# Attention products of 256 columns: from whole fp32 operands to two parts each and three single-pass matmuls

## The chip, the cores and the metric

One core of a Trainium2 chip runs the whole program. The metric is the device time of one execution in microseconds (us), as the median of several runs; one further execution is taken by the hardware profiler, and all rows below come from that one.

## The reference, cut to what matters

A decoder trunk of two layers over 256 tokens with a model width of 2048 and 16 heads of 128. Layer 0 has 8 stick-breaking heads and 8 dilated-window heads, layer 1 has 16 forgetting heads. All arrays are float32.

```python
def forgetting_attention(q, k, v, log_f):          # layer 1, all 16 heads
    s = einsum('bqhd,bkhd->bhqk', qblk, k) * scale
    s = s + cq[..., None] - c[:, :, None, :]
    s = where(kpos[None, :] <= qpos[:, None], s, -inf)
    return einsum('bhqk,bkhd->bqhd', softmax(s), v)

def stick_breaking_attention(q, k, v):             # layer 0, heads 0 to 7
    z = einsum('bqhd,bkhd->bhqk', qblk, k) * scale
    w = exp(log_sigmoid(z) + suffix)               # strictly causal
    return einsum('bhqk,bkhd->bqhd', w, v)
# layer 0, heads 8 to 15: a softmax over a mixture of dilated windows

for i in range(DEPTH):
    a = rmsnorm(h, attn_norm[i])
    h = h + mixer(a)                               # w_in, attention, w_out
    h = h + conv_ffn(rmsnorm(h, ffn_norm[i]), ...) # w_up, conv, w_down
    gate = sigmoid(rmsnorm(h, ple_norm[i]) @ w_ple_gate[i])
    h = h + gate * (p[i] @ w_ple[i])
return rmsnorm(h, final_norm)
```

## The kernel before

All activations lie in SBUF with features on the partitions and the 256 tokens as columns. The weights (453 MB) are streamed from HBM once. They are cut into 882 units, mostly of 4 blocks of 128x256 numbers. For each unit ScalarE rounds the raw weights to the single-pass type float32r (the high part, L176) and VectorE subtracts that from the raw weights (the low part, L177). The activations have two such parts as well. A product is then three single-pass matmuls of 256 columns (high by high, high by low, low by high; `PARTS`, L206 and L215), so a unit of four blocks is 24 matmuls. Units are split three ahead of their use (`LOOK`), into four buffers. In the value projection (`gemm_v`, L249) the roles are swapped: the activations are the stationary operand and the weights stream.

The heads are taken in pairs, eight pairs in each layer. `head_pair` emits four units each for q, k and v. Each unit ends in `tick()`, and small pieces of work are put between units by `defer(n, fn)`, which runs `fn` n units later. For each pair three such pieces run, while the next pair's projections stream:

- `first`: the scores. Of each head the causal blocks are one product of 128 columns (L435 in `sb_first`, L480 in `sm_first`) and one of 256 columns (L438, L482). They take q and k whole, as float32. In layer 1 a bias product of 384 columns in float32r comes before them (L478).
- `second`, four or five units later: `sb_second` (suffix sums by L456 to L464, single-pass, then Exp on ScalarE at L467) or `sm_second` (six transposes of 128 columns by TensorE at L517, then one copy to SBUF by ScalarE at L519).
- `attend`, two units later: the products of weights and values, again one of 128 columns (L526) and one of 256 (L529) for each of the two heads, all whole.

The values are copied out of PSUM by ScalarE with the row norm as a factor (L618, L585), the scores' q and k by VectorE (L590, L593). `t2_tile` gives one of six buffers of 128x512 floats. The engines' queues are in order: TensorE runs the scores exactly between the units where `defer` put them, and ScalarE and VectorE run the attention's steps between the splits of weights.

A float32 matmul is recorded as two instructions, each of which is a weight load (PEld) and a matmul (PE); a float32r matmul is recorded as one of each.

Of the kernel before, what the change touches and what calls it, by code (L numbers as in the profile page):

```python
# [17 lines left out]
P = 128  # L18
D = 2048
S = 256  # L20
# [84 lines left out]
def trunk(ctx: ExitStack, tc: tile.TileContext, xT, pT, pos, gains, conv, bf, cst, wst, out):  # L105
# [17 lines left out]
    acc = cpool.tile([P, 2, S], F32, name="acc")  # L123
    rb = cpool.tile([P, S], F32, name="rb")
    rq = cpool.tile([P, S], F32, name="rq")
    rT = cpool.tile([P, 2], F32, name="rT")

    root = cpool.tile([P, 2], F32, name="root")
    nc.gpsimd.memset(root, -0.5)

    ident = ct[:, C_ID:C_ID + 128]
# [62 lines left out]
    def defer(n, fn):  # L194
        later.append((at["tick"] + n, fn))
# [233 lines left out]
        nc.vector.tensor_add(out=x[:32], in0=x[:32], in1=sw)  # L429


    def sb_first(q, k):
        sc = at_tile("scs")
        for j in range(2):
            nc.tensor.matmul(sc[:, 1, j * P:(j + 1) * P], lhsT=k[:, j, 128:256], rhs=q[:, j, 128:256],  # L435
                             start=j == 0, stop=True, skip_group_check=True)
        for j in range(2):
            nc.tensor.matmul(sc[:, 0, j * S:(j + 1) * S], lhsT=k[:, j, 0:128], rhs=q[:, j, :],  # L438
                             start=j == 0, stop=True, skip_group_check=True)
        z, e = t3_tile("z"), t3_tile("e")  # L440
        for i, (a, b) in enumerate(((0, 256), (256, 384))):
            msk = ct[:, C_MSB + a:C_MSB + b].unsqueeze(1).to_broadcast([P, 2, b - a])
            nc.vector.tensor_add(out=z[:, 2 * a:2 * b].rearrange("p (j c) -> p j c", j=2),
                                 in0=sc[:, i, 0:2 * (b - a)].rearrange("p (j c) -> p j c", j=2), in1=msk)
        nc.vector.scalar_tensor_tensor(out=e, in0=z, scalar=-1.0, in1=z, op0=ALU.mult, op1=ALU.min)
        nc.scalar.activation(out=e, in_=e, func=AF.Exp)
        nc.scalar.activation(out=e, in_=e, func=AF.Ln, bias=1.0)
        nc.vector.scalar_tensor_tensor(out=e, in0=z, scalar=0.0, in1=e, op0=ALU.max, op1=ALU.add)
        eh, el = t3_tile("eh", (P, 768), F32R), t3_tile("el", (P, 768), F32R)
        nc.scalar.copy(out=eh, in_=e)  # L450
        nc.vector.tensor_sub(out=el, in0=e, in1=eh.bitcast(F32))
        return z, e, eh, el

    def sb_second(z, e, eh, el):
        sp = at_tile("sps")
        nc.tensor.matmul(sp[:, 0, :], lhsT=trir[:, 1, :], rhs=eh[:, 0:512],  # L456
                         start=True, stop=False, skip_group_check=True)
        for i, x in enumerate((eh, el)):
            nc.tensor.matmul(sp[:, 1, 0:256], lhsT=trir[:, 1, :], rhs=x[:, 512:768],
                             start=i == 0, stop=i == 1, skip_group_check=True)  # L460
            nc.tensor.matmul(sp[:, 0, :].rearrange("p (j c) -> p j c", j=2)[:, :, 128:256],
                             lhsT=trir[:, 0, :], rhs=x[:, 512:768].rearrange("p (j c) -> p j c", j=2),
                             start=False, stop=False, skip_group_check=True)
        nc.tensor.matmul(sp[:, 0, :], lhsT=trir[:, 1, :], rhs=el[:, 0:512],  # L464
                         start=False, stop=True, skip_group_check=True)
        nc.vector.tensor_sub(out=z, in0=z, in1=sp.rearrange("p a b -> p (a b)")[:, :768])
        nc.scalar.activation(out=e, in_=z, func=AF.Exp)  # L467
        return e

    SEG = ((0, 128), (128, 384))  # L470

    def sm_first(q, k, fox):
        sc = at_tile("scs")
        for j in range(2):
            if fox is not None:
                c2, sel, cq, h0 = fox
                lh = sel[:, h0 + j:h0 + j + 1].to_broadcast([P, P])
                nc.tensor.matmul(sc[:, j, 0:384], lhsT=lh, rhs=c2, start=True, stop=False,  # L478
                                 skip_group_check=True)
            nc.tensor.matmul(sc[:, j, 0:128], lhsT=q[:, j, 0:128], rhs=k[:, j, 0:128],  # L480
                             start=fox is None, stop=True, skip_group_check=True)
            nc.tensor.matmul(sc[:, j, 128:384], lhsT=q[:, j, 128:256], rhs=k[:, j, :],  # L482
                             start=False, stop=True, skip_group_check=True)
        s, pe = t3_tile("s", (P, 2, 384)), t3_tile("pe", (P, 2, 384))
        if fox is None:
            msk = ct[:, C_MDL:C_MDL + 384].unsqueeze(1).to_broadcast([P, 2, 384])
            nc.vector.tensor_add(out=s, in0=sc[:, :, :384], in1=msk)
        else:
            for j in range(2):
                for t, (a, b) in enumerate(SEG):  # L490
                    nc.vector.scalar_tensor_tensor(
                        out=s[:, j, a:b], in0=sc[:, j, a:b], scalar=cq[:, t, h0 + j:h0 + j + 1],
                        in1=ct[:, C_MFX + a:C_MFX + b], op0=ALU.add, op1=ALU.add)
        mx = work.tile([P, 2, 2], F32, name="mx", tag="mx", bufs=2)
        sm = work.tile([P, 2, 2], F32, name="sm", tag="sm", bufs=2)
        rsm = work.tile([P, 2, 2], F32, name="rsm", tag="rsm", bufs=2)
        for t, (a, b) in enumerate(SEG):
            nc.vector.tensor_reduce(out=mx[:, t, :], in_=s[:, :, a:b], axis=AX.X, op=ALU.max,
                                    negate=True)
        for j in range(2):  # L500
            for t, (a, b) in enumerate(SEG):
                nc.scalar.activation(out=pe[:, j, a:b], in_=s[:, j, a:b], func=AF.Exp,
                                     bias=mx[:, t, j:j + 1], accum_out=sm[:, t, j:j + 1])
        nc.vector.reciprocal(out=rsm, in_=sm)
        for t, (a, b) in enumerate(SEG):
            for j in range(2):
                nc.vector.tensor_scalar_mul(out=pe[:, j, a:b], in0=pe[:, j, a:b],
                                            scalar1=rsm[:, t, j:j + 1])
        return pe, s

    def sm_second(pe, s):

        sp = at_tile("sps")
        for j in range(2):
            for i in range(3):
                o = sp[:, 0, j * S + i * P:j * S + (i + 1) * P] if i < 2 else sp[:, 1, j * P:(j + 1) * P]
                nc.tensor.transpose(out=o, in_=pe[:, j, i * P:(i + 1) * P], identity=ident)  # L517
        w = s.rearrange("p a b -> p (a b)")
        nc.scalar.copy(out=w, in_=sp.rearrange("p a b -> p (a b)")[:, :768])  # L519
        return w  # L520

    def attend(hp, w, v, dst):
        av = at_tile("avp")
        for j in range(2):
            js = slice(j * P, (j + 1) * P)
            nc.tensor.matmul(av[:, 0, j * S + 128:(j + 1) * S], lhsT=v[:, 1, js],  # L526
                             rhs=w[:, 512 + j * P:512 + (j + 1) * P], start=j == 0, stop=False,
                             skip_group_check=True)
            nc.tensor.matmul(av[:, 0, j * S:(j + 1) * S], lhsT=v[:, 0, js], rhs=w[:, j * S:(j + 1) * S],  # L529
                             start=False, stop=True, skip_group_check=True)  # L530
        parts(dst[:, 2 * hp:2 * hp + 2], av[:, 0, :].rearrange("p (j s) -> p j s", j=2))


# [42 lines left out]
    def head_pair(l, hp, act, dst, st):  # L576
        q = work.tile([P, 2, S], F32, name="q", tag="qkv", bufs=2)
        k = work.tile([P, 2, S], F32, name="k", tag="qkv", bufs=2)
        v = work.tile([P, 2, S], F32, name="v", tag="v", bufs=1)
        full = _cuts(KT)  # L580
        if l % 2 == 1 and hp == 0:
            ps = at_tile("psv")
            gemm_vf(ps, act, l)
            for t in range(2):
                nc.scalar.activation(out=v[:, t, :], in_=ps[:, t, 0:S], func=AF.Copy,  # L585
                                     scale=rT[:, t:t + 1])
            st["fox"] = forget_gates(l, ps)
        ps = mm_tile("psq")
        gemm(ps, act, "w_in", l, hp * 256, full)
# [5 lines left out]

        def first():
            if l % 2 == 0 and hp < 4:
                a = sb_first(q, k)
                defer(5, lambda: second(lambda: sb_second(*a)))
            else:  # L600
                a = sm_first(q, k, st["fox"] + (2 * hp,) if l % 2 == 1 else None)
                defer(4, lambda: second(lambda: sm_second(*a)))

        def second(fn):
# [3 lines left out]
        if l % 2 == 0 and hp >= 4:  # L608
            rope(q)
            rope(k)  # L610

        defer(late + (2 + (l % 2 == 0 and hp >= 4) if hp == 7 or (l % 2 == 1 and hp == 0) else 4), first)
        if l % 2 == 1 and hp == 0:
            return
        ps = mm_tile("psv")
        gemm_v(ps, act, l, 2 * D + hp * 256)
        for i in range(2):
            nc.scalar.activation(out=v[:, i, :], in_=ps[:, i, :], func=AF.Copy, scale=rT[:, i:i + 1])  # L618

    def ffn_group(l, g, g0, act, hid):  # L620
        c = [t2_tile("yg"), t2_tile("yv")]
# [206 lines left out]
```

## Time and profile before

| | us |
|---|---|
| median of three runs | 2422.91 (2422.68 to 2423.42) |
| the profiled execution's own time | 2423.48 |
| its span, first to last instruction | 2421.7 |
| TensorE matmuls busy | 2407.1 (99%) |
| VectorE busy | 1581.5 (65%) |
| ScalarE busy | 1227.9 (51%) |
| granted TensorE clock, share of 2.4 GHz | 0.998 |

A matmul's recorded duration is a latency: the next one starts long before it ends. What a matmul costs the stream is the spacing of the ends, and the chain of waits gives that: each of its pieces is a stretch of one kind of work with a count, and the length over the count is the spacing.

### The profile page before, as it was taken

The numbers are of one execution on the slowest core, as the hardware profiler recorded it, in microseconds if no ns is written. First come the engines' busy times: TensorE is split into PE (matmuls) and PEld (weight loads), VectorE is DVE, ScalarE is ACT, GpSimd is POOL, SyncE is SP. The second block draws the span as 40 slices with busy tenths as digits, with TensorE's granted clock in tenths as the row PEclk, the third lists the DMA queues.
The fourth block names the chain that finished last, engine by engine and source line by source line (L and its number), as shares of the span: only waits on it lengthen the run. The fifth ranks groups of instructions, "written<-read, shape, count | busy, mean of one in ns | idle before, by whom it ended". The sixth has DMA issues, their size and how long they took to land.

```text
span 2421.7 us, 47927 instructions
## 1 busy us (share of the span) xinstructions
PE 2407.1 (99%) x20992; PEld 2401.0 (99%) x20992; DVE 1581.5 (65%) x2066; ACT 1227.9 (51%) x1546; POOL 5.8 (0%) x13
## 2 busy tenths in 40 slices
PE   9999999999999999999999999999999999999998
PEld 9999999999999999999999999999999999999997
DVE  7666766776567657767755555667665776567666
ACT  6554455554355445555554444555544554455554
POOL 0000000000000000000000000000000000000000
PEclk9999999999999999999999999999999999999999
DMA  7454455555555555555555454555555555555553
GB/s 285 166 181 172 174 182 192 192 192 194 197 197 196 187 197 192 193 186 202 184 188 173 167 181 163 199 190 194 192 192 193 192 196 191 201 194 187 186 202 122
DMA packets 66818, 458.05 MB, mean 189 GB/s; under 512 B 7552, under 2 KB 7840, under 8 KB 16944
## 3 DMA queue, kind: packets, MB, share of 16 engines
q1 hardware_dynamic: 66576, 454.93, 53.3%
q8 instruction: 164, 2.69, 0.4%
q14 instruction: 46, 0.38, 0.0%
q0 software_dynamic: 32, 0.06, 0.0%
HBM read 452.86 MB, written 2.10 MB: 188 GB/s over the span
## 4 chain that ended last, share of the span: by engine, by line
PE 99%; DVE 0%; DMA 0%; ACT 0%; issue 0%; SPq 0%; POOLq 0%; DVEq 0%; ACTq 0%
PE psu L215 40%; PE psd L215 20%; PE psk L215 7%; PE psq L215 7%; PE pso L215 7%; PE psv L249 7%; PE psg L215 7%; PE avp L529 1%; PE psv L262 0%; PE psp L215 0%; PE pse L726 0%; PE scs L482 0%; PE sps L517 0%; PE avp L526 0%; DMA h<-in_x 0%; PE scs L480 0%
## 5 line engine op out<-in xcount | busy, mean ns | idle before, releaser
L177 DVE TENSOR_TENSOR w<-wr,w 128x1024 fp32r<-128x1024 f32 (+2 forms) x874 | 1045.6, 1198 | 687.2 <-ACT w L176 683.2
L176 ACT CAST w<-wr 128x1024 fp32r<-128x1024 f32 (+2 forms) x874 | 900.9, 1031 | 1065.5 <-PE psu L215 354.5
L215 PE MATMUL psu<-act,w 128*128 128x256 f32 x8448 | 959.7, 276 | 0.0
L215 PEld LDWEIGHTS psu<-act,w 128*128 128x128 f32 x8448 | 958.4, 188 | 0.1
L215 PE MATMUL psd<-act,w 128*128 128x256 f32 x4224 | 479.7, 276 | 0.0
L215 PEld LDWEIGHTS psd<-act,w 128*128 128x128 f32 x4224 | 479.2, 188 | 0.0
L215 PE MATMUL psk<-act,w 128*128 128x256 f32 x1536 | 184.3, 279 | 0.0
L215 PE MATMUL psq<-act,w 128*128 128x256 f32 x1536 | 182.6, 279 | 0.9 <-DVE w L177 0.9
L215 PEld LDWEIGHTS psk<-act,w 128*128 128x128 f32 x1536 | 179.5, 188 | 0.8
L215 PEld LDWEIGHTS psq<-act,w 128*128 128x128 f32 x1536 | 178.4, 188 | 1.7 <-DVE w L177 1.2
L215 PE MATMUL pso<-act,w 128*128 128x256 f32 x1536 | 176.5, 277 | 0.0
L215 PEld LDWEIGHTS pso<-act,w 128*128 128x128 f32 x1536 | 175.6, 188 | 0.1
L249 PE MATMUL psv<-w,act 128*128 128x256 f32 x1440 | 167.0, 277 | 0.0
L249 PEld LDWEIGHTS psv<-w,act 128*128 128x128 f32 x1440 | 165.2, 188 | 0.1
L215 PE MATMUL psg<-act,w 128*128 128x256 f32 x1440 | 164.8, 276 | 0.0
L215 PEld LDWEIGHTS psg<-act,w 128*128 128x128 f32 x1440 | 163.9, 188 | 0.1
L627 DVE TENSOR_TENSOR u<-psu,rb 128x512 f32<-128x512 f32 x88 | 60.9, 692 | 33.0 <-PE psu L215 32.8
L633 DVE SCALAR_TENSOR_TENSOR yg<-u,cv,yg 128x256 f32<-128x256 f32 x176 | 73.3, 478 | 0.0
L633 DVE SCALAR_TENSOR_TENSOR yv<-u,cv,yv 128x256 f32<-128x256 f32 x176 | 73.3, 478 | 0.0
L630 ACT ACTIVATE yg<-u,cv 128x256 f32<-128x256 f32 x88 | 48.0, 593 | 1.1 <-DVE u L627 1.1
L630 ACT ACTIVATE yv<-u,cv 128x256 f32<-128x256 f32 x88 | 48.0, 593 | 0.0
L273 ACT CAST act<-yg 128x512 fp32r<-128x512 f32 x44 | 27.3, 621 | 38.8 <-DVE yg L643 38.8
(165 smaller groups left out, 883.5 us busy)
## 6 DMA issues: line engine op xcount, KB each, us to landing
wr<-in_w SPq DMA_DIRECT2D x388, 1024.0 KB, 4.8
wr<-in_w SPq DMA_DIRECT2D x36, 768.0 KB, 4.3
wr<-in_w SPq DMA_DIRECT2D x8, 896.0 KB, 4.6
h<-in_x SPq DMA_DIRECT2D x4, 512.0 KB, 8.9
wr<-in_w SPq DMA_DIRECT2D x4, 512.0 KB, 10.0
out_dram<-h SPq DMA_DIRECT2D x7, 256.0 KB, 2.4
wr<-in_w SPq DMA_DIRECT2D x2, 816.0 KB, 4.4
pl<-in_w SPq DMA_DIRECT2D x3, 512.0 KB, 7.8
```

The source lines that it names most:

```text
L176: nc.scalar.copy(out=w[:, :, 0, :], in_=raw)
L177: nc.vector.tensor_sub(out=w[:, :, 1, :], in0=raw, in1=w[:, :, 0, :].bitcast(F32))
L215: nc.tensor.matmul(ps[:, j, :], lhsT=w[:, k, s, js], rhs=act[:, k0 - koff + k, t, :], start=first and j + k + n == 0, stop=last and k == k ...
L249: nc.tensor.matmul(ps[:, t], lhsT=act[:, 4 * i + k, a, tsl], rhs=w[:, k, b], start=i + t + k + n == 0, stop=i == 3 and k == kc - 1 and n = ...
L273: nc.scalar.copy(out=dst[:, :, 0, :], in_=src)
L529: nc.tensor.matmul(av[:, 0, j * S:(j + 1) * S], lhsT=v[:, 0, js], rhs=w[:, j * S:(j + 1) * S], start=False, stop=True, skip_group_check=True)
L627: nc.vector.tensor_mul(out=u[:, :, 2:], in0=ps, in1=rb2)
L630: nc.scalar.activation(out=y[:, j, :], in_=u[:, j, 2:], func=AF.Identity, bias=cv[:, l, t, 3:4], scale=cv[:, l, t, 2:3])
L633: nc.vector.scalar_tensor_tensor(out=y[:, j, :], in0=u[:, j, tap:tap + S], scalar=cv[:, l, t, tap:tap + 1], in1=y[:, j, :], op0=ALU.mult, ...
```

## The change

The products of 256 columns of scores and values take both operands in two parts and become three single-pass matmuls, as the projections are. The products of 128 columns stay whole.

- `prepare` runs once q and k of a pair are in SBUF and makes the parts: of the streaming operand (q in `sb_first`, k in `sm_first`) all 256 columns of both heads (`in_parts`: a ScalarE copy and a VectorE subtraction of 128x512), of the stationary one 128 columns of both heads (`tile_parts`: the same of 128x256).
- `sb_second` and `sm_second` return the attention weights of the 256 columns in two parts (`in_parts`), and those of the other 128 columns whole. In `sm_second` the copy of 768 columns becomes a copy of 512, a subtraction of 512 and a copy of 256.
- `values` makes the parts of the first 128 tokens' values by one more VectorE instruction of 128x256.
- Two small tiles become one, and the value tile is split in a tile of parts and a whole one. In SBUF there are 1 KB more for each partition, and 32 bytes fewer from the merged tile.

```diff
@@ -123,9 +123,9 @@
     acc = cpool.tile([P, 2, S], F32, name="acc")
     rb = cpool.tile([P, S], F32, name="rb")
     rq = cpool.tile([P, S], F32, name="rq")
-    rT = cpool.tile([P, 2], F32, name="rT")
-
-    root = cpool.tile([P, 2], F32, name="root")
+    rr = cpool.tile([P, 4], F32, name="rr")
+    rT, root = rr[:, 0:2], rr[:, 2:4]
+
     nc.gpsimd.memset(root, -0.5)
 
     ident = ct[:, C_ID:C_ID + 128]
@@ -429,14 +429,30 @@
         nc.vector.tensor_add(out=x[:32], in0=x[:32], in1=sw)
 
 
-    def sb_first(q, k):
+
+
+    def in_parts(x, name):
+        hi, lo = t2_tile(name + "h", dt=F32R), t2_tile(name + "l", dt=F32R)
+        nc.scalar.copy(out=hi, in_=x)
+        nc.vector.tensor_sub(out=lo, in0=x, in1=hi.bitcast(F32))
+        return hi, lo
+
+    def tile_parts(x):
+        xp = t2_tile("xp", (P, 2, 2, P), F32R)
+        nc.scalar.copy(out=xp[:, 0], in_=x)
+        nc.vector.tensor_sub(out=xp[:, 1], in0=x, in1=xp[:, 0].bitcast(F32))
+        return xp[:, 0], xp[:, 1]
+
+    def sb_first(q, k, prepared):
+        full, one = prepared
         sc = at_tile("scs")
         for j in range(2):
             nc.tensor.matmul(sc[:, 1, j * P:(j + 1) * P], lhsT=k[:, j, 128:256], rhs=q[:, j, 128:256],
                              start=j == 0, stop=True, skip_group_check=True)
         for j in range(2):
-            nc.tensor.matmul(sc[:, 0, j * S:(j + 1) * S], lhsT=k[:, j, 0:128], rhs=q[:, j, :],
-                             start=j == 0, stop=True, skip_group_check=True)
+            for n, (a, b) in enumerate(PARTS):
+                nc.tensor.matmul(sc[:, 0, j * S:(j + 1) * S], lhsT=one[a][:, j, :], rhs=full[b][:, j, :],
+                                 start=j + n == 0, stop=n == 2, skip_group_check=True)
         z, e = t3_tile("z"), t3_tile("e")
         for i, (a, b) in enumerate(((0, 256), (256, 384))):
             msk = ct[:, C_MSB + a:C_MSB + b].unsqueeze(1).to_broadcast([P, 2, b - a])
@@ -465,11 +481,12 @@
                          start=False, stop=True, skip_group_check=True)
         nc.vector.tensor_sub(out=z, in0=z, in1=sp.rearrange("p a b -> p (a b)")[:, :768])
         nc.scalar.activation(out=e, in_=z, func=AF.Exp)
-        return e
+        return in_parts(e[:, 0:512].rearrange("p (j s) -> p j s", j=2), "w"), e[:, 512:768]
 
     SEG = ((0, 128), (128, 384))
 
-    def sm_first(q, k, fox):
+    def sm_first(q, k, prepared, fox):
+        full, one = prepared
         sc = at_tile("scs")
         for j in range(2):
             if fox is not None:
@@ -479,8 +496,9 @@
                                  skip_group_check=True)
             nc.tensor.matmul(sc[:, j, 0:128], lhsT=q[:, j, 0:128], rhs=k[:, j, 0:128],
                              start=fox is None, stop=True, skip_group_check=True)
-            nc.tensor.matmul(sc[:, j, 128:384], lhsT=q[:, j, 128:256], rhs=k[:, j, :],
-                             start=False, stop=True, skip_group_check=True)
+            for n, (a, b) in enumerate(PARTS):
+                nc.tensor.matmul(sc[:, j, 128:384], lhsT=one[a][:, j, :], rhs=full[b][:, j, :],
+                                 start=False, stop=n == 2, skip_group_check=True)
         s, pe = t3_tile("s", (P, 2, 384)), t3_tile("pe", (P, 2, 384))
         if fox is None:
             msk = ct[:, C_MDL:C_MDL + 384].unsqueeze(1).to_broadcast([P, 2, 384])
@@ -515,19 +533,30 @@
             for i in range(3):
                 o = sp[:, 0, j * S + i * P:j * S + (i + 1) * P] if i < 2 else sp[:, 1, j * P:(j + 1) * P]
                 nc.tensor.transpose(out=o, in_=pe[:, j, i * P:(i + 1) * P], identity=ident)
-        w = s.rearrange("p a b -> p (a b)")
-        nc.scalar.copy(out=w, in_=sp.rearrange("p a b -> p (a b)")[:, :768])
-        return w
+        w = in_parts(sp[:, 0, :].rearrange("p (j s) -> p j s", j=2), "w")
+        w1 = s.rearrange("p a b -> p (a b)")[:, 0:256]
+        nc.scalar.copy(out=w1, in_=sp[:, 1, 0:256])
+        return w, w1
+
+    def values(v, t, ps):
+
+        if t == 0:
+            nc.scalar.activation(out=v[0][:, 0, :], in_=ps, func=AF.Copy, scale=rT[:, 0:1])
+            nc.vector.scalar_tensor_tensor(out=v[0][:, 1, :], in0=ps, scalar=rT[:, 0:1],
+                                           in1=v[0][:, 0, :].bitcast(F32), op0=ALU.mult, op1=ALU.subtract)
+        else:
+            nc.scalar.activation(out=v[1], in_=ps, func=AF.Copy, scale=rT[:, 1:2])
 
     def attend(hp, w, v, dst):
+        w, w1 = w
         av = at_tile("avp")
         for j in range(2):
             js = slice(j * P, (j + 1) * P)
-            nc.tensor.matmul(av[:, 0, j * S + 128:(j + 1) * S], lhsT=v[:, 1, js],
-                             rhs=w[:, 512 + j * P:512 + (j + 1) * P], start=j == 0, stop=False,
-                             skip_group_check=True)
-            nc.tensor.matmul(av[:, 0, j * S:(j + 1) * S], lhsT=v[:, 0, js], rhs=w[:, j * S:(j + 1) * S],
-                             start=False, stop=True, skip_group_check=True)
+            nc.tensor.matmul(av[:, 0, j * S + 128:(j + 1) * S], lhsT=v[1][:, js], rhs=w1[:, j * P:(j + 1) * P],
+                             start=j == 0, stop=False, skip_group_check=True)
+            for n, (a, b) in enumerate(PARTS):
+                nc.tensor.matmul(av[:, 0, j * S:(j + 1) * S], lhsT=v[0][:, a, js], rhs=w[b][:, j, :],
+                                 start=False, stop=n == 2, skip_group_check=True)
         parts(dst[:, 2 * hp:2 * hp + 2], av[:, 0, :].rearrange("p (j s) -> p j s", j=2))
 
 
@@ -576,14 +605,13 @@
     def head_pair(l, hp, act, dst, st):
         q = work.tile([P, 2, S], F32, name="q", tag="qkv", bufs=2)
         k = work.tile([P, 2, S], F32, name="k", tag="qkv", bufs=2)
-        v = work.tile([P, 2, S], F32, name="v", tag="v", bufs=1)
+        v = (work.tile([P, 2, S], F32R, name="vp", tag="vp"), work.tile([P, S], F32, name="v", tag="v"))
         full = _cuts(KT)
         if l % 2 == 1 and hp == 0:
             ps = at_tile("psv")
             gemm_vf(ps, act, l)
             for t in range(2):
-                nc.scalar.activation(out=v[:, t, :], in_=ps[:, t, 0:S], func=AF.Copy,
-                                     scale=rT[:, t:t + 1])
+                values(v, t, ps[:, t, 0:S])
             st["fox"] = forget_gates(l, ps)
         ps = mm_tile("psq")
         gemm(ps, act, "w_in", l, hp * 256, full)
@@ -595,10 +623,10 @@
 
         def first():
             if l % 2 == 0 and hp < 4:
-                a = sb_first(q, k)
+                a = sb_first(q, k, st["parts"])
                 defer(5, lambda: second(lambda: sb_second(*a)))
             else:
-                a = sm_first(q, k, st["fox"] + (2 * hp,) if l % 2 == 1 else None)
+                a = sm_first(q, k, st["parts"], st["fox"] + (2 * hp,) if l % 2 == 1 else None)
                 defer(4, lambda: second(lambda: sm_second(*a)))
 
         def second(fn):
@@ -608,6 +636,15 @@
         if l % 2 == 0 and hp >= 4:
             rope(q)
             rope(k)
+
+        def prepare():
+
+            if l % 2 == 0 and hp < 4:
+                st["parts"] = in_parts(q, "f"), tile_parts(k[:, :, 0:128])
+            else:
+                st["parts"] = in_parts(k, "f"), tile_parts(q[:, :, 128:256])
+
+        with_rows(prepare)
 
         defer(late + (2 + (l % 2 == 0 and hp >= 4) if hp == 7 or (l % 2 == 1 and hp == 0) else 4), first)
         if l % 2 == 1 and hp == 0:
@@ -615,7 +652,7 @@
         ps = mm_tile("psv")
         gemm_v(ps, act, l, 2 * D + hp * 256)
         for i in range(2):
-            nc.scalar.activation(out=v[:, i, :], in_=ps[:, i, :], func=AF.Copy, scale=rT[:, i:i + 1])
+            values(v, i, ps[:, i, :])
 
     def ffn_group(l, g, g0, act, hid):
         c = [t2_tile("yg"), t2_tile("yv")]
```

## Rows read from the trace of the kernel before

**Rows 1.** The page: busy time by engine, and the chain that ended last by engine.
```profile
PE 2407.1 (99%) x20992; PEld 2401.0 (99%) x20992; DVE 1581.5 (65%) x2066; ACT 1227.9 (51%) x1546; POOL 5.8 (0%) x13
...
PE 99%; DVE 0%; DMA 0%; ACT 0%; issue 0%; SPq 0%; POOLq 0%; DVEq 0%; ACTq 0%
```

**Rows 2.** The chain of waits in order: start us, length us, engine, tile, line, count.
```profile
42.40 10.88 PE psv L249 x96
...
1218.87 8.48 PE psq L215 x72
```

**Rows 3.** Groups of TensorE instructions by form: busy us, mean ns of one | idle us.
```profile
L529 PE MATMUL avp<-s,v 128*128 128x256 f32 x48 | 14.3, 380 | 0.0
L482 PE MATMUL scs<-k,q 128*128 128x256 f32 x48 | 14.3, 380 | 0.0
...
L529 PE MATMUL avp<-e,v 128*128 128x256 f32 x16 | 4.8, 380 | 0.0
...
L438 PE MATMUL scs<-q,k 128*128 128x256 f32 x16 | 4.1, 380 | 0.0
```

**Rows 4.** The chain in the first head pairs (stick-breaking), 60 to 130 us.
```profile
85.69 0.12 PE sps L459
...
89.66 0.87 PE scs L438 x4
90.53 2.83 PE psq L215 x24
...
112.83 0.43 PE avp L529 x2
113.26 2.74 PE psk L215 x24
```

**Rows 5.** The chain around transposes and values of a softmax pair, 205 to 225 us.
```profile
211.55 0.66 PE sps L517 x6
212.21 5.66 PE psk L215 x48
...
218.52 0.22 PE avp L526 x2
...
219.18 5.46 PE psk L215 x48
```

**Rows 6.** Stretches with attention, L215's instructions, then L249's: length, busy us, count.
```profile
70.40:407.30 336.90, 239.89 (x2043) 1.00 0.50 178
1246.00:1608.80 362.80, 264.56 (x2249) 1.00 0.51 178
...
70.40:407.30 336.90, 78.05 (x672) 1.00 0.50 178
```

**Rows 7.** Groups of ScalarE and VectorE instructions by form: busy us, mean ns | idle us.
```profile
L519 ACT COPY s<-sps 128x768 f32<-128x768 f32 x12 | 9.5, 792 | 0.0
...
L273 ACT CAST act<-avp 128x512 fp32r<-128x512 f32 x16 | 9.4, 587 | 3.7 <-PE avp L529 3.7
...
L283 DVE SCALAR_TENSOR_TENSOR act<-h,gn,act 128x256 fp32r<-128x256 f32 x96 | 41.8, 478 | 0.3 <-ACT act L281 0.3
...
L274 DVE TENSOR_TENSOR act<-avp,act 128x512 fp32r<-128x512 f32 x16 | 10.9, 684 | 0.0
...
L322 DVE COPY rb<-rps 128x256 f32<-128x256 f32 x6 | 2.5, 421 | 3.4 <-PE rps L319 3.4
```

**Rows 8.** Waits: who waited for whom, us in total, times, longest us.
```profile
ACT w L176 <- PE psk L215: 97.6, 54, 3.0
```

**Rows 9.** Timeline of ScalarE, then TensorE, at the fourth pair's values: start us, us.
```profile
182.07 0.85 ACT L467 ACTIVATE e<-z 128x768 f32<-128x768 f32 x1
...
184.25 0.39 PE L526 MATMUL avp<-e,v 128*128 128x128 f32 x2
```

**Rows 10.** Timeline of VectorE, then TensorE, at layer 1's first scores: start us, us.
```profile
1242.34 0.69 DVE L593 TENSOR_TENSOR k<-psk,rb 128x512 f32<-128x512 f32 x1 [0.41 <-PE psk L215]
...
1246.40 0.27 PE L480 MATMUL scs<-k,q 128*128 128x128 f32 x1
```

## Prediction

> **What bounds the kernel.** I read the page first, then the chain of waits in order of time, then the groups by form, and last the waits and two timelines. The page says that TensorE is busy for 2407.1 of 2421.7 us and that the chain that ended last is 99% TensorE [rows 1]. So only what changes TensorE's own stream, or makes it wait, moves the time. The recorded 380 ns of a matmul [rows 3] are a latency and no price; the price is the spacing in the chain.
>
> The reader is to see two spacings there. A stretch of 96 projection matmuls takes 10.88 us, 113.3 ns each; another of 72 takes 8.48 us, 117.8 ns each [rows 2]. The forms are equal, and the granted clock is 1.00 in both attention stretches [rows 6], so this is no clock. I call them the fast and the slow rate; they differ by 4.5 ns. The slow rate begins after an interruption of the stream by something else than a projection and then lasts for whole units. After the six transposes of a softmax pair the next 48 matmuls take 5.66 us (117.9 ns); after the values of 256 columns the next 48 take 5.46 us (113.8 ns) [rows 5]. I went through the chain and listed all such pieces: after the transposes 11 of 12 are slow, after the values 0 of 16, after the scores 4 of 16 (one is the piece at 90.53, 2.83 us for 24 [rows 4]). What makes the rate I can't read from the trace, only where it changes.
>
> **The removed products.** Rows 3 give 48 + 48 + 16 + 16 = 128 records of whole products of 256 columns; a whole one is two records, so 64 matmuls are replaced. Each costs 434 ns: 0.87 us for four records, 0.43 for two [rows 4]. The products of 128 columns, 0.22 us for two records [rows 5], stay.
>
> **The added products.** Each becomes three single-pass matmuls. The low bound is the fast rate, 3 x 113.3 = 340 ns, the high bound the 0.12 us of a single-pass matmul in an odd surrounding (the suffix sums at 85.69 [rows 4]), 360 ns. I take 117 each, 351 ns, since they come right behind a product of 128 columns in two passes, and a stream that follows two-pass work starts slowly: 24 matmuls after the values take 2.74 us where 24 x 113.3 is 2.72 [rows 4]. Saved: 64 x (434 - 351) ns = 5.3 us, with 4.7 and 6.0 as bounds. The slow start that the projections now have behind the 32 groups of scores and values (about 15 ns, by the same row) falls into the new products: 0.4 us more. Together 5.7 us, if the projections keep their rates.
>
> A load of a stationary operand comes with each single-pass matmul, and a rule bears on that. The rows have it that loads and matmuls run side by side, for both are busy 99% of the span [rows 1]. The Trainium skill, "TensorE: Matmul & The Clock Gate", gives in its section on the back-to-back gap N / 2.4 + 2.5 ns, 109 ns for 256 columns, and in that on LDWEIGHTS the columns over 1.2, 107 ns for 128. By that page the sum would be an estimated 64 x (434 - 327) ns = 6.8 us. The trace has no matmul of this form at 109, so the rate in the rows decides.
>
> **The added work on ScalarE and VectorE.** A copy of 128x512 by ScalarE takes 0.59 us, a subtraction by VectorE 0.68; a 128x256 VectorE instruction takes 0.42 to 0.48 [rows 7]. For a pair VectorE gets two subtractions of 512, one of 256 and one for the values: 2 x 0.68 + 0.42 + 0.48 = 2.3 us, 16 x 2.3 = 36 us in all. For a 256-column copy on ScalarE I estimate 0.4 from the 0.59 of 512. Then a stick-breaking pair adds two copies of 512 and one of 256, 1.6 us; a softmax pair adds one of each for the scores and turns the 0.79 us copy into 0.59 + 0.4, 1.2 us. With 4 and 12 pairs that is 21 us. VectorE goes from 65% to 67%, ScalarE from 51% to 52%. What hides it is that the splits run ahead: ScalarE waits 97.6 us in 54 places for TensorE to free a weight buffer, behind the key projections alone [rows 8], so a split that comes 1 us later still comes before its unit. Cost: nothing. If that cover were gone, each late split would stop TensorE for up to the 1.3 us that one pair's `prepare` adds to VectorE's queue at a time (0.68 + 0.42, and an estimated 0.2 of overheads and waiting).
>
> **The added waits.** TensorE's queue is in order, so a late part stops the projections behind it. Two places are tight. At the fourth pair the Exp ends at 182.92 and the values begin at 184.25, 1.33 us later [rows 9]; the high part needs 0.59 us, the low part another 0.68, together 1.27. The low part is first read by the fifth instruction of the group, some 0.35 us after its start (the two records of 128 columns, then the product of high parts). So it fits with 0.4 us to spare, unless a split of about 1 us gets between; behind VectorE's subtraction stand the splits, which have their lead. At layer 1's first scores k is ready at 1243.03 and the 128-column scores begin at 1246.40 [rows 10]; 0.59 + 0.68 + 0.42 and one split ahead of it fit into 3.4 us. I take 0.2 us for all of this, bounds 0 and 3 (about 1 us at three such places).
>
> **The sum.** 5.7 - 0.2 = 5.5 us. The profiled execution goes from a span of 2421.7 to 2416.2 (2423.48 to 2418.0 with what lies around it); its time is 0.6 above the median, so the median goes from 2422.9 to 2417.4. Its own range, from 4.7 to 6.4 saved and up to 1 us of waits, is 2416.5 to 2419.2. A measurement of this kernel can tell about 0.2%, 4.8 us, from no change, so this forecast lies just beyond that line.
>
> **Rivals.**
>
> *The slow rate spreads (slower).* Now the groups of scores and values end in two-pass products of 256 columns, and behind these the stream is mostly fast. After the change each ends in single-pass products that directly follow two-pass ones of 128 columns, and the nearest thing to that in the trace is the group of transposes, behind which 11 of 12 pieces are slow [rows 5]. The attention stretches hold 2043 + 2249 matmuls of L215 and 672 of L249 in each of the two, 5636 together [rows 6]. The slow pieces that I listed there count 852. If all the other 4784 became slow, that would cost 4784 x 4.5 ns = 21.5 us: the products then save 64 x (434 - 354) ns = 5.1 us, and the time is 2422.9 - 5.1 + 21.5 = 2439. If half did, 2428.6. It decides from 5.5 / 0.0045 = 1200 matmuls on, a quarter of them. For it: the transposes; and that the slow rate, once there, goes on through several units without an interruption [rows 2]. Against it: the next group of another kind mostly ends it; the single-pass suffix sums are followed by the fast rate in 3 of 4 pairs; and the new products carry no transposes.
>
> *The slow rate goes.* If the stream never slows behind scores, values or transposes, the 852 are freed: 3.8 us more, 2413.6.
>
> *Waits eat it.* If parts come late at the four stick-breaking pairs and at layer 1's first pair by about 1 us each, 5 us are lost: 2422.4. It speaks for this that the margin is 0.4 us in one place, against it that the other places have more.
>
> *The change doesn't do what it says.* If three single-pass matmuls with these operands cost no less than the two-pass product, 145 ns each, nothing is won: 2423. No single-pass matmul of 256 columns in the attention stretches is near that.
>
> **How the numbers follow.** Forecast 0.43; the slow rate spreads 0.33, in a weak form (up to 1200 or so more slow matmuls and some beyond, between -4.8 and +4.8 us) 0.13 and in a strong one 0.20; the slow rate goes 0.09; waits 0.10; no gain per product 0.05. Faster by over 0.2% is 0.75 of the forecast (0.32) and the slow rate's going (0.09), 0.41. Slower by over 0.2% is the strong spread and 0.05 of combinations with waits, 0.25. Within 0.2% is the rest, 0.34. The range: low 2413.5, where the second rival lies; high 2430, a little over the half of the spread; above it I leave some 0.13. The likeliest case's own range is 2416.5 to 2419.2.
>
> **What would show it.** In the chain of the changed kernel a group of values for two heads should take 2 x (0.22 + 0.35) us in place of 2 x (0.22 + 0.43). The projections behind it are right at 2.72 to 2.74 us for 24 and wrong at 2.83. TensorE's idle time before the new products should be 0.0; a wait of it on VectorE or ScalarE at `attend` in the stick-breaking pairs would be the third rival. VectorE's busy time should rise by 36 us, ScalarE's by 21. The prediction is wrong if more than some 1200 further projection matmuls run at the slow rate, or if the new products take over 0.43 us for three.

## The result, and the profile after

The changed kernel takes 2436.84 us (2435.41 to 2437.22) against 2423.42 us of the kernel before on the same chip: a ratio of 1.0051, interval [1.0039, 1.0062]. It is slower by 13.4 us, where 5.5 us less were forecast; the time is near the price of the first rival with all of its matmuls, 2439.

The page of the profile after, TensorE's share and the chain by engine, stands as in [rows 1]:

```profile
PE 2417.8 (99%) x21056; PEld 2414.8 (99%) x21056; DVE 1613.2 (66%) x2130; ACT 1245.2 (51%) x1593; POOL 5.9 (0%) x13
...
PE 98%; DVE 1%; ACT 0%; issue 0%; DMA 0%; SPq 0%; POOLq 0%; DVEq 0%; ACTq 0%
```

TensorE is as full as before, and its work has become longer. (What the prediction calls a two-pass product is a whole float32 product, which the trace records as two matmuls; the text below says "whole".) The chain around the same softmax pair as in [rows 5], from 210 to 242 us of the changed kernel, shows where (start us, length us, engine, tile, line, count; L497 and L555 are the products of 128 columns, L500 and L558 the single-pass ones):

```profile
215.49 0.66 PE sps L535 x6
216.14 5.46 PE psk L215 x48
221.60 0.22 PE avp L555 x2
221.82 0.36 PE avp L558 x3
222.18 0.22 PE avp L555 x2
222.40 0.35 PE avp L558 x3
222.75 5.65 PE psk L215 x48
228.40 11.30 PE psv L249 x96
```

Three single-pass matmuls take 0.35 to 0.36 us where the whole product took 0.43, as worked out. Behind the values, though, 48 projection matmuls take 5.65 us in place of 5.46, and the 96 of the value projection take 11.30 in place of 10.88. And behind the transposes it is the other way round: 5.46 us where rows 5 have 5.66; that comes with the merged tile and not with the products, as before_shifted shows below. So in the softmax pairs the slow rate now begins at the values, and the next transposes end it. At the last values of layer 0 nothing ends it for a long time. The chain there, 322 to 421 us:

```profile
329.67 76.32 PE pso L215 x648
...
414.81 5.57 PE psu L215 x48
```

The 648 matmuls of the output projection run at 117.8 ns each, and so do the 72 behind them (8.48 us), until the row norm's small products at 414 us interrupt the stream.

A count of the spacings in the whole trace, between neighbours of one line, has 1141 slow matmuls (between 115 and 124 ns, the 272-column ones left out) before and 4477 after: 3336 more, at 4.5 ns each 15.0 us. (Counted over the lines L215 and L249 alone it is 1119 and 4472; for no kernel of the table below do the two ways differ by more than 25.) The products themselves save 0.15 us in each of 32 groups (0.22 + 0.36 + 0.22 + 0.35 = 1.15 us against 2 x (0.22 + 0.43) = 1.30), 4.8 us. The rest is waiting, which the view of TensorE's waits shows:

```profile
PE avp L558 <- ACT wh L436: 1.0, 1, 1.0
PE avp L555 <- ACT e L483: 0.3, 1, 0.3
```

Together 15.0 - 4.8 + 1.3 = 11.5 of the 13.1 us between the spans; 0.9 more lie at the start, ahead of every changed product, where the first query projection's first matmul ends at 20.42 us in place of 19.51 (18.71 in before_shifted: this differs from trace to trace), and some 0.7 are not assigned.

The wait is that of the second pair's values. The chain there, 103 to 120 us, and under it ScalarE's and VectorE's timelines:

```profile
112.43 0.84 ACT e L483
...
114.11 0.62 ACT wh L436
...
114.78 0.39 PE avp L558
115.17 1.16 PE psk L215 x10
116.33 0.29 PE avp L558 x2
```

```profile
107.54 1.28 ACT L418 ACT_TABLE_LOAD   x1
...
109.91 0.28 DVE L421 TENSOR_SCALAR angn<-angn 32x256 f32<-32x256 f32 x1
110.12 0.94 DVE L482 TENSOR_TENSOR z<-z,sps 128x768 f32<-128x768 f32 x1
```

The rotary tables (L401 to L422) are computed just there, on both engines, ahead of the pair's Exp; the high part of its weights, `wh`, comes behind a weight cast and is ready at 114.73 us. Ten projection matmuls stand inside the value group: the order of TensorE's instructions has them between the first single-pass matmul and the others, in this group alone.

### The profile page after: what moved, and what is told of

It reads as the page before. It is cut to its first block, busy times and chain, and to the rows that moved or that the text cites. A ratio compares the mean times of both kernels' runs of the same rounds, so it can differ in the third digit from the quotient of the medians.

```text
span 2434.8 us, 48170 instructions
## 1 busy us (share of the span) xinstructions
PE 2417.8 (99%) x21056; PEld 2414.8 (99%) x21056; DVE 1613.2 (66%) x2130; ACT 1245.2 (51%) x1593; POOL 5.9 (0%) x13
## 4 chain that ended last, share of the span: by engine, by line
PE 98%; DVE 1%; ACT 0%; issue 0%; DMA 0%; SPq 0%; POOLq 0%; DVEq 0%; ACTq 0%
PE psu L215 39%; PE psd L215 20%; PE pso L215 7%; PE psk L215 7%; PE psq L215 7%; PE psv L249 7%; PE psg L215 7%; PE psp L215 1%; PE psv L262 0%; PE avp L558 0%; PE pse L763 0%; PE scs L500 0%; PE sps L535 0%; PE avp L555 0%; DVE w L177 0%
## 5 line engine op out<-in xcount | busy, mean ns | idle before, releaser
L215 PE MATMUL psu<-act,w 128*128 128x256 f32 x8448 | 960.3, 276 | 0.0
L215 PEld LDWEIGHTS psu<-act,w 128*128 128x128 f32 x8448 | 959.0, 188 | 0.1
L215 PE MATMUL psd<-act,w 128*128 128x256 f32 x4224 | 479.7, 276 | 0.0
L215 PEld LDWEIGHTS psd<-act,w 128*128 128x128 f32 x4224 | 479.2, 188 | 0.0
L215 PE MATMUL psq<-act,w 128*128 128x256 f32 x1536 | 183.5, 280 | 1.0 <-DVE w L177 1.0
L215 PE MATMUL psk<-act,w 128*128 128x256 f32 x1536 | 183.5, 279 | 0.0
L215 PEld LDWEIGHTS psq<-act,w 128*128 128x128 f32 x1536 | 180.3, 189 | 1.3 <-DVE w L177 1.2
L215 PE MATMUL pso<-act,w 128*128 128x256 f32 x1536 | 181.3, 281 | 0.0
L215 PEld LDWEIGHTS pso<-act,w 128*128 128x128 f32 x1536 | 180.6, 189 | 0.0
L215 PEld LDWEIGHTS psk<-act,w 128*128 128x128 f32 x1536 | 180.2, 188 | 0.1
L249 PE MATMUL psv<-w,act 128*128 128x256 f32 x1440 | 171.7, 279 | 0.0
L249 PEld LDWEIGHTS psv<-w,act 128*128 128x128 f32 x1440 | 170.2, 188 | 0.0
L215 PE MATMUL psg<-act,w 128*128 128x256 f32 x1440 | 164.8, 276 | 0.0
L215 PEld LDWEIGHTS psg<-act,w 128*128 128x128 f32 x1440 | 163.9, 188 | 0.1
```

What stands on the lines that cost most here:

```text
L215: nc.tensor.matmul(ps[:, j, :], lhsT=w[:, k, s, js], rhs=act[:, k0 - koff + k, t, :], start=first and j + k + n == 0, stop=last and k == k ...
L249: nc.tensor.matmul(ps[:, t], lhsT=act[:, 4 * i + k, a, tsl], rhs=w[:, k, b], start=i + t + k + n == 0, stop=i == 3 and k == kc - 1 and n = ...
```

## The experiments

Three theories stood against each other. A: what a group of products between the projections consists of, and in which order, sets the rate of the projections behind it. B: the merged tile shifts all work tiles by 32 bytes, and the addresses set the rate. C: the added work of ScalarE and VectorE slows TensorE. The times of a row of the table are medians, each beside the kernel before on the same chip; "slow" is the count of slow matmuls as above.

| kernel | us | ratio to before [interval] | slow |
|---|---|---|---|
| before | 2423.42 | | 1141 |
| changed | 2436.84 | 1.0051 [1.0039, 1.0062] | 4477 |
| values_whole | 2423.56 | 1.0000 [0.9990, 1.0009] | 669 |
| scores_whole | 2438.62 | 1.0064 [1.0049, 1.0079] | 4738 |
| values_grouped | 2420.16 | 0.9986 [0.9976, 0.9995] | 791 |
| before_shifted | 2423.42 | 1.0001 [0.9992, 1.0010] | 1135 |
| whole_behind | 2426.28 | 1.0014 [1.0004, 1.0024] | 715 |
| values_three_last | 2435.59 | 1.0052 [1.0037, 1.0067] | 4496 |
| both_grouped | 2418.40 | 0.9980 [0.9970, 0.9989] | 443 |
| both_rope_later | 2415.47 | 0.9968 [0.9956, 0.9979] | 407 |
| one_single_more | 2422.08 | 0.9995 [0.9985, 1.0004] | 615 |
| two_singles_more | 2440.12 | 1.0064 [1.0047, 1.0081] | 4930 |
| three_singles_more | 2425.31 | 1.0004 [0.9995, 1.0014] | 884 |
| before_rope_later | 2424.19 | 1.0001 [0.9991, 1.0010] | 1357 |

### Half of the change each

values_whole: `attend`, `values` and the returned weights as before (one place of the diff shown).

```diff
...
-            for n, (a, b) in enumerate(PARTS):
-                nc.tensor.matmul(av[:, 0, j * S:(j + 1) * S], lhsT=v[0][:, a, js], rhs=w[b][:, j, :],
-                                 start=False, stop=n == 2, skip_group_check=True)
+            nc.tensor.matmul(av[:, 0, j * S:(j + 1) * S], lhsT=v[:, 0, js], rhs=w[:, j * S:(j + 1) * S],
+                             start=False, stop=True, skip_group_check=True)
```

> The changed kernel with its value products whole again; only the scores of 256 columns are in parts. Theory A (what a group of products between the projections ends in, and in which order, sets the rate of the projections behind it): behind the values the fast rate comes back, so some 3300 of the 4477 slow matmuls of the changed kernel go; the scores keep 32 x 83 ns = 2.7 us of gain: about 2420.5 us, ratio to the kernel before 0.9975 to 1.000. Theory B (the 32-byte shift of the work tiles' addresses sets the rate): as slow as the changed kernel, 2434 or more. Theory C (the added work on ScalarE and VectorE slows TensorE's reads, about in proportion): half of the loss, near 2430.

scores_whole: `sb_first` and `sm_first` as before, no `prepare` (one place of the diff shown).

```diff
...
-            for n, (a, b) in enumerate(PARTS):
-                nc.tensor.matmul(sc[:, j, 128:384], lhsT=one[a][:, j, :], rhs=full[b][:, j, :],
-                                 start=False, stop=n == 2, skip_group_check=True)
+            nc.tensor.matmul(sc[:, j, 128:384], lhsT=q[:, j, 128:256], rhs=k[:, j, :],
+                             start=False, stop=True, skip_group_check=True)
```

> The changed kernel with its scores whole again; only the value products of 256 columns are in parts. Theory A: the projections behind every group of values run at the slow rate until the next scores or transposes, and to the end of the output projection behind the last values of a layer: some 3000 more slow matmuls than before, 13 to 14 us, less 2.6 us: 2432 to 2436, ratio 1.004 to 1.005. Theory B: 2434 or more as well. Theory C: half of the loss, near 2430.

The chain behind the same pair's values, first of values_whole, then of scores_whole:

```profile
222.47 0.43 PE avp L550 x2
222.90 5.46 PE psk L215 x48
228.36 10.88 PE psv L249 x96
```

```profile
224.15 0.35 PE avp L554 x3
224.50 5.65 PE psk L215 x48
230.16 11.30 PE psv L249 x96
```

With the values whole the rate is fast and the loss is gone; with the values in parts alone the loss is there in full. So the value group does it, and the work on the other engines does not: theory C would have split the loss, and values_grouped (below) does the same work on them without it. scores_whole came out above its range of 2432 to 2436: its bias scores, whole again, leave the slow rate behind them 8 times of 8. The gain of the scores, 2.4 us by their groups, does not show in values_whole's time; its trace has 2.6 us of TensorE waiting for weights at the key projections in two places, which the changed kernel's does not have, and I did not follow them up.

### Addresses

before_shifted: the kernel before with the merged tile of the diff's first part.

```diff
-    rT = cpool.tile([P, 2], F32, name="rT")
-    root = cpool.tile([P, 2], F32, name="root")
+    rr = cpool.tile([P, 4], F32, name="rr")
+    rT, root = rr[:, 0:2], rr[:, 2:4]
```

> The kernel before with only the two small tiles merged, which shifts the addresses of all work tiles by 32 bytes; no product is changed. Theory A and C: 2423, ratio 0.9995 to 1.0005, slow matmuls as before (1141). Theory B: the slow rate in most of the attention stretches, 2434 or more.

No difference in the time, and 1135 slow matmuls against 1141: as the cause of the loss, theory B falls. But the slow matmuls no longer stand in the same places. The chain in before_shifted at the transposes of [rows 5], and behind the bias scores of layer 1's second pair:

```profile
211.30 0.65 PE sps L517 x6
211.96 5.46 PE psk L215 x48
...
1282.31 8.48 PE psq L215 x72
```

In the kernel before, the same 72 matmuls are fast:

```profile
1283.44 8.16 PE psq L215 x72
```

Behind the transposes 0 of 12 pieces are slow where 11 were, and behind the bias scores all 8 where 2 were; behind the values none of 16 in either. In each of the twelve kernels with the merged tile the projections behind all 12 transposes are fast. So the merge does change the rate at some places, and the equal count is a coincidence. Whether the value groups in parts would leave the same rates at other addresses is not shown: every kernel that has them has the merged tile.

### The order within the group

values_grouped: both products of 128 columns first, then the six single-pass matmuls.

```diff
                              start=j == 0, stop=False, skip_group_check=True)
+        for j in range(2):
+            js = slice(j * P, (j + 1) * P)
             for n, (a, b) in enumerate(PARTS):
```

> The changed kernel with another order in the value group alone: both products of 128 columns first, then the six single-pass matmuls (the order that the stick-breaking scores have, behind which the changed kernel's trace shows the fast rate 4 times of 4). Theory A, if the order decides: the fast rate behind all values, 2417 to 2421, ratio 0.997 to 0.999. If what decides is only that a group ends in single-pass matmuls: no change against the changed kernel, 2436. Theories B and C: 2436 too.

The chain behind the same values:

```profile
221.03 0.44 PE avp L555 x4
221.47 0.72 PE avp L560 x6
222.19 5.45 PE psk L215 x48
```

The same products in another order leave the fast rate behind them 15 times of 16; the exception is the second pair, whose group has projections inside. The time is now under that of the kernel before, though the second pair still waits.

whole_behind: one whole product of 256 columns more behind the changed group, unused.

```diff
+        nc.tensor.matmul(av[:, 1, 0:S], lhsT=v[1][:, 0:P], rhs=v[1], start=True, stop=True,
+                         skip_group_check=True)
```

> The changed kernel with one whole product of 256 columns more behind each group of values, into an unused part of the group's PSUM buffer; nothing reads its result. Theory A1 (what a group ends in sets the rate): behind it the fast rate is back, 3300 slow matmuls or some 15 us less, and 16 x 0.44 = 7.0 us more: 2428 to 2430. Rival A2 (the alternation of the two kinds inside the group sets it, whatever comes behind): 2436.8 + 7 = 2444.

values_three_last: three single-pass matmuls, both products of 128 columns, three single-pass matmuls. `three(j, first)` issues the three of head j; its definition and the removed lines are left out here.

```diff
...
+        three(0, True)
+        for j in range(2):
+            js = slice(j * P, (j + 1) * P)
+            nc.tensor.matmul(av[:, 0, j * S + 128:(j + 1) * S], lhsT=v[1][:, js], rhs=w1[:, j * P:(j + 1) * P],
+                             start=False, stop=False, skip_group_check=True)
+        three(1, False)
```

> The changed kernel with another order in the value group alone: three single-pass matmuls, both products of 128 columns, three single-pass matmuls. So the group ends as in the changed kernel, with three single-pass matmuls behind a product of 128 columns, but it changes from two passes to a single one once, as the grouped order does. A1 (three single-pass matmuls behind two passes leave the slow rate, six don't): 2435 to 2438. A2 (one change from two passes to one is harmless, two are not): 2419 to 2421.

The chain behind the last products, first of whole_behind, then of values_three_last:

```profile
221.55 0.43 PE avp L560 x2
221.98 5.47 PE psk L215 x48
```

```profile
220.71 0.35 PE avp L557 x3
221.06 5.65 PE psk L215 x48
```

What the group ends in decides, not the alternation: a whole product at the end, which costs 16 x 0.43 = 6.9 us, brings 10.6 us net, and one change of kind with three single-pass matmuls at the end is slow behind all 16 groups and within 1.3 us of the changed kernel.

### How many single-pass matmuls at the end

one_single_more, two_singles_more and three_singles_more: the changed group with m = 1, 2 or 3 unused single-pass matmuls behind it, so that 4, 5 or 6 follow the last whole product.

```diff
+        for i in range(m):
+            nc.tensor.matmul(av[:, 1, 0:S], lhsT=v[0][:, 0, 0:P], rhs=w[0][:, 0, :], start=True, stop=True,
+                             skip_group_check=True)
```

> The changed kernel with one single-pass matmul of 256 columns more behind each group of values (four behind the last two-pass product in place of three), into an unused part of the group's PSUM buffer; nothing reads its result. It costs 16 x 0.118 = 1.9 us. If the number must reach six: slow behind the values as before, 2438 to 2439. If an even number is what leaves the fast rate: 15 us less, 2423 to 2425. If any longer run helps gradually: between.

> The same with two more (five behind the last two-pass product), 3.8 us more of work. If the number must reach six, or be even: 2440 to 2441. If four or five are enough: 2425 to 2427.

> The same with three more (six behind the last two-pass product, as in the grouped order, but with the alternation left in), 5.7 us more of work. If the number of single-pass matmuls behind the last two-pass product decides: 2426 to 2428. If it is something else in the grouped order (four two-pass products in a row, or the same buffers one behind the other): 2442.

The chain in the three, with the added matmuls (L561) and the projections behind them:

```profile
220.17 0.12 PE avp L561
220.29 5.45 PE psk L215 x48
```

```profile
223.05 0.24 PE avp L561 x2
223.29 5.65 PE psk L215 x48
```

```profile
221.78 0.36 PE avp L561 x3
222.14 5.44 PE psk L215 x48
```

Three and five at the end leave the slow rate behind all 16 groups, four the fast one behind all 16, six behind 15: the second pair's, with ten projections inside, leaves the slow rate there. So the length of the run is not what matters, nor any slack that it gives: one more matmul makes the kernel faster by 14.8 us (2422.08 against 2436.84), the next one slower by 18.0. At the end of this group, for the four numbers tried, it is whether their number is odd or even. The two fast kernels came out about 1 us under their ranges, and whole_behind 2 us.

### The scores' order, and the second pair's wait

both_grouped: the order of values_grouped in `sm_first` too (that place of the diff shown).

```diff
                              start=fox is None, stop=True, skip_group_check=True)
+        for j in range(2):
             for n, (a, b) in enumerate(PARTS):
```

> The changed kernel with the grouped order in the values and in the softmax scores (both products of 128 columns, with the bias products ahead of them, then the six single-pass matmuls). If the order works at the scores as it does at the values, the slow stretches behind the softmax scores go as well (some 290 matmuls in layer 0 and 180 in layer 1): 1 to 2 us less than with the values alone, 2418 to 2419. If it does nothing there: 2420.2.

The chain behind a softmax pair's scores, first of values_grouped (its last piece cut by the window, 117.7 ns each), then of both_grouped:

```profile
239.31 0.35 PE scs L500 x3
239.67 10.36 PE psq L215 x88
```

```profile
237.25 0.72 PE scs L501 x6
237.97 10.89 PE psq L215 x96
```

both_rope_later: besides, the rotary tables 8 units later (that place shown).

```diff
-                rope_tables()
+                defer(8, rope_tables)
```

> As the one before, and the rotary tables are computed 8 units later, behind the second pair's values, so that VectorE's and ScalarE's work for them no longer stands between that pair's suffix sums and its Exp. The second pair's value group then waits no longer (1.0 + 0.7 us of TensorE's waiting in the trace of the grouped values): 2416 to 2418, faster than the kernel before by 0.2 to 0.3%. If that wait was only moved: as the one before.

TensorE's waits at a value group, 1.0 and 0.7 us in both_grouped's trace,

```profile
PE avp L556 <- ACT e L483: 1.0, 1, 1.0
...
PE avp L561 <- ACT wh L436: 0.7, 1, 0.7
```

are gone in that of both_rope_later, whose second pair's group runs without a gap:

```profile
111.10 0.45 PE avp L556 x4
111.54 0.72 PE avp L561 x6
112.26 2.73 PE psk L215 x24
```

This version takes 2415.47 us, 0.32% less than the kernel before, and is the fastest of all: 4.8 us less for the products and (1141 - 407) x 4.5 ns = 3.3 us less at the slow rate make 8.1, against 8.0 measured. How much of the 3.3 comes with the merged tile, which alone ends the slow rate behind the transposes and brings it behind the bias scores, is not taken apart.

before_rope_later: the same move in the kernel before, alone.

> The kernel before with the rotary tables 8 units later and nothing else. If the second pair's values wait for the tables' work only because of the parts that the change adds: 2423, as before. If the kernel before loses time there as well: up to 1 us less.

There it brings nothing, so the wait came with the parts.

## Why the prediction was wrong

**The products.** Right, a little too good. Saved were 0.15 us for each group, 4.8 us in all, near the low bound of 4.7, where the sum had 5.3 + 0.4. Each three take 350 to 360 ns where 351 was taken, and the slow start that was to come on top of that (0.4 us in all; 32 x 15 ns is nearer to 0.5) is mostly within it.

**The projections' rate.** This is the step that failed, "if the projections keep their rates". The list behind it was right: after the values 0 of 16 pieces were slow. But those groups ended in a whole product of 256 columns, and the change takes just that away; whole_behind puts it back, and the fast rate with it. The forecast carried the list over to groups that no longer ended so: the term for the projections behind them was put at nothing (beyond a 0.4 us gain), and they cost 15.0 us. The first rival had the effect, the place and the price (1200 matmuls to break even, 2439 with all of them); 3336 came. It got 0.20 in its strong form. That the time came so near its 2439 is in part luck: 3336 matmuls and not 4784 turned slow, 6.5 us less than priced, and 2.9 us of waits, later start and what is not assigned made up for some of it. Its reason does not hold either. It leaned on the transposes, slow behind them 11 times of 12; but these change with the merged tile alone (0 of 12 in before_shifted), and single-pass matmuls behind products of 128 columns leave the slow or the fast rate, as their number has it. And it came behind the values, 16 times of 16, but not behind all scores: behind the stick-breaking ones 4 of 4 pieces are fast.

**ScalarE and VectorE.** Right in what they cost, a little high in size: 31.7 us more for VectorE (36 said) and 17.3 for ScalarE (21 said), hidden but for one place.

**The waits.** Within the bounds, but in another place: 1.3 us of waiting where 0.2 were taken, with 3 as the bound. The fourth pair, with 0.4 us to spare, waits for nothing; the second, where the rotary tables stand ahead of the Exp, waits. I looked at two margins, the fourth pair's and that of layer 1's first scores, and took them for the tightest, without asking what else runs on the two engines at the others.

**The other rivals.** The slow rate's going was priced by the 852 slow pieces; the changed kernel does not do it, but with the grouped order at both places the count falls from 1141 to 443, and to 407 with the rotary tables moved. That the products would cost as much as before is refuted by their 0.35 us.

## What to carry to other kernels

When TensorE is the bound, a change of a few short products is priced by them and by the stream behind them: 4.8 us of products were outweighed by 15 us in matmuls that the change did not touch. A stretch of equal matmuls should be read by its spacing, before and after each interruption, and where two spacings show, the order within the interrupting group is worth a try: it costs no work, and here it turned +13.4 us into -3.0, and the same order at the scores and one moved block of table work into -8.0. And slow stretches should be compared place by place: two kernels with 1141 and 1135 of them had them behind different groups.

## What the runs showed of the hardware

Back-to-back single-pass matmuls of 256 columns run at two rates at the same granted clock (1.00 in the attention stretches of both kernels), 113.3 and 117.8 ns, and keep the one that they start with over hundreds of instructions, 648 in the output projection. Not always: in the changed kernel's layer 0 the rate goes from slow to fast without other products between, where the output projection takes over from the value projection.

```profile
311.39 2.83 PE psv L249 x24
314.22 8.18 PE pso L215 x72
```

Behind this kernel's value groups, where no projections stand inside them, the rate went by whether an odd (3, 5) or even (4, 6) number of single-pass matmuls followed the last whole product. That is shown for these groups at these addresses alone. The scores of the dilated-window heads, which also end in three, turn the rate from fast to slow 4 times of 4 in values_whole's trace. But the bias scores, which end in three too, mostly keep the rate that they came with: in values_whole's trace 7 of 8 stay fast, in the changed kernel's 7 stay slow and 1 fast. And in both_grouped two of the 16 score groups, which all end in six, leave the slow rate: the two that stand inside a value projection. Behind the transposes the rate is mostly the opposite of the one ahead of them in the kernel before (9 of 12 from fast to slow); with the merged tile it is fast in all 12, whatever it was (9 of 12 from slow to fast in the changed kernel, 10 of 12 fast on both sides in both_grouped). Behind the stick-breaking scores, which end in six, the changed kernel goes from the slow to the fast rate (152 to 179 us):

```profile
155.30 11.30 PE psv L249 x96
...
167.04 0.71 PE scs L454 x6
167.75 10.88 PE psq L215 x96
```

What it is in the engine that has two states, and why 32 bytes bear on it at some groups, stays open: no record of the trace other than the spacing tells the rates apart.
